# Rotary embedding on one core: the adds of five pieces moved from TensorE to VectorE, and pieces of 6, 5 and 5 positions in place of 4

## The chip, the cores and the metric

The kernel runs on one core of a Trainium2 chip. The metric is device microseconds from launch to end; the profile's span, from the first to the last instruction, is about 1.8 us shorter. Runs are sorted into fast and slow ones: a run more than 1.5% above the fastest of its kernel counts as slow.

## The reference

```python
# x: (8, 2048, 8, 64) float32; cos, sin: (2048, 32) float32
x1 = x[..., :32]
x2 = x[..., 32:]
out1 = x1 * cos - x2 * sin        # cos, sin broadcast over batch and heads
out2 = x1 * sin + x2 * cos
return np.concatenate([out1, out2], axis=-1)
```

Every element is read once and written once, 33.55 MB each way, for three arithmetic operations per output element: two products and an add.

## The kernel before

Each of the 128 partitions holds 16 consecutive sequence positions, so one batch is a tile of 128 x 8192 elements, 512 (8 heads of 64) per position. Five such tiles are kept (`NBUF = 5`), and the result is written over the input. A tile is worked on in pieces of a few positions. SBUF and PSUM are two on-chip memories: the tiles lie in SBUF, and TensorE's results go to PSUM. In most pieces (kind A) GpSimd multiplies the swapped halves by the signed sines (`t2`), VectorE multiplies by the cosines (`t1`, in PSUM), and VectorE adds. To relieve VectorE, three pieces (kind B) are added on TensorE: two matmuls with the identity into one PSUM bank (the tile `o` of 512 elements), copied out ("evicted") by ScalarE. To relieve GpSimd too, two pieces (kind C) take both products on VectorE and the add on TensorE.

```python
kinds = {}
for b, kind in ((1, "C"), (2, "B"), (3, "C"), (4, "B"), (5, "B")):
    kinds[(b, 0)] = kind
# ...
if kind != "C":
    keep(nc.gpsimd.tensor_mul(out=t2..., in0=swapped(xt, nr), in1=signed(sgn[...], nr)))
keep(nc.vector.tensor_mul(out=t1..., in0=xk, in1=rep(cos_ps[...], 2 * H)))
if kind == "A":
    keep(nc.vector.tensor_add(out=xt, in0=t1, in1=t2))
elif kind == "B":
    for j in range(n // C):
        o = o_pool.tile([P, C], f32, tag="o")
        cs = slice(j * C, (j + 1) * C)
        nc.tensor.matmul(o, eye, t1[:, cs], start=True, stop=False)
        nc.tensor.matmul(o, eye, t2[:, cs], start=False, stop=True)
        keep(nc.scalar.copy(xt[:, cs], o))
# ... kind C: second product on VectorE, then as B with +-identity

# per batch: pieces of 4 positions ([2, 2, 4, 4, 4] in the first, [4, 4, 4, 2, 2] in the last),
# one store per batch (three in the first and the last: 8, 4, 4 positions), then:
if b + NBUF <= last:
    load(b + NBUF)          # waits until the store of batch b has landed
```

Of the kernel before, what the change touches and what calls it, by code (L numbers as in the profile page):

```python
# [9 lines left out]
@with_exitstack  # L10
def kernel(
    ctx: ExitStack,
    tc: tile.TileContext,
    x: bass.AP,
    cos: bass.AP,
    sin: bass.AP,
    out: bass.AP,
):
    nc = tc.nc
    keep = tc.keep_in_program_order  # L20
    f32 = mybir.dt.float32
    PSUM = bass.MemoryType.PSUM

    B, S, H, D = x.shape
    Dh = D // 2
    P = 128
    HD = H * D
    R = S // P
    ROW = R * HD
    UNIT = 4 * HD  # L30
    NBUF = 5
    C = 512
    last = B - 1

    xv = x.rearrange("b (q r) h d -> b q (r h d)", q=P)
    ov = out.rearrange("b (q r) h d -> b q (r h d)", q=P)
    cos_src = cos.rearrange("(q r) d -> q r d", q=P)
    sin_src = sin.rearrange("(q r) d -> q r d", q=P)

    const_pool = ctx.enter_context(tc.tile_pool(name="const", bufs=1))  # L40
    tab_pool = ctx.enter_context(tc.tile_pool(name="tab", bufs=1, space=PSUM))
    t1_pool = ctx.enter_context(tc.tile_pool(name="t1p", bufs=1, space=PSUM))
    o_pool = ctx.enter_context(tc.tile_pool(name="op", bufs=2, space=PSUM))
    t1s_pool = ctx.enter_context(tc.tile_pool(name="t1s", bufs=2))
    xpool = ctx.enter_context(tc.tile_pool(name="xpool", bufs=NBUF))
    t2_pool = ctx.enter_context(tc.tile_pool(name="t2p", bufs=3))

    cos_sb = t1s_pool.tile([P, R, Dh], f32, tag="t1s", name="cos_sb")
    sin_sb = t1s_pool.tile([P, R, Dh], f32, tag="t1s", name="sin_sb")
    sgn = const_pool.tile([P, R, 2, Dh], f32, tag="sg")  # L50
    eye = const_pool.tile([P, P], f32, tag="eye")
    neye = const_pool.tile([P, P], f32, tag="neye")
    cos_ps = tab_pool.tile([P, R, Dh], f32, tag="cp")
    sin_ps = tab_pool.tile([P, R, Dh], f32, tag="sp")

    xts = {}

    def spans(sizes):
        lo = 0
        for n in sizes:  # L60
            yield lo, n
            lo += n

    def load(b):
        xt = xpool.tile([P, ROW], f32, tag="xt", name=f"xt{b}")
        for lo, n in spans([UNIT, UNIT, 2 * UNIT] if b == 0 else [ROW]):
            keep(nc.sync.dma_start(out=xt[:, lo : lo + n], in_=xv[b, :, lo : lo + n]))  # L67
            if b == 0 and lo == 0:
                keep(nc.sync.dma_start(out=cos_sb, in_=cos_src))  # L69
                keep(nc.sync.dma_start(out=sin_sb, in_=sin_src))  # L70
        xts[b] = xt

    def store(b, lo, n):
        keep(nc.scalar.dma_start(out=ov[b, :, lo : lo + n], in_=xts[b][:, lo : lo + n]))  # L74

    for b in range(NBUF):
        load(b)

    nc.gpsimd.memset(eye, 0.0)  # L79
    nc.gpsimd.affine_select(  # L80
        out=eye,
        in_=eye,
        compare_op=mybir.AluOpType.not_equal,
        fill=1.0,
        base=0,
        pattern=[[-1, P]],
        channel_multiplier=1,
    )
    for lo, hi in ((0, 4), (4, R)):
        keep(nc.scalar.mul(sgn[:, lo:hi, 0, :], sin_sb[:, lo:hi, :], -1.0))  # L90
        keep(nc.scalar.copy(sgn[:, lo:hi, 1, :], sin_sb[:, lo:hi, :]))  # L91
    keep(nc.scalar.copy(sin_ps, sin_sb))  # L92
    keep(nc.scalar.mul(neye, eye, -1.0))
    keep(nc.vector.tensor_copy(cos_ps, cos_sb))  # L94

    def rep(a, n):
        return dataclasses.replace(a, ap=[a.ap[0][:], a.ap[1][:], [0, n], a.ap[-1][:]])

    def swapped(a, nr):
        return dataclasses.replace(  # L100
            a,
            offset=a.offset + Dh,
            ap=[a.ap[0][:], [HD, nr], [D, H], [-Dh, 2], [1, Dh]],
        )

    def signed(a, nr):
        return dataclasses.replace(
            a, ap=[a.ap[0][:], [D, nr], [0, H], [Dh, 2], [1, Dh]]
        )

    kinds = {}
    for b, kind in ((1, "C"), (2, "B"), (3, "C"), (4, "B"), (5, "B")):
        kinds[(b, 0)] = kind

    def rotate(b, lo, n):
        kind = kinds.get((b, lo), "A")
        xt = xts[b][:, lo : lo + n]
        r0 = lo // HD
        nr = n // HD
        xk = xt.rearrange("p (r k d) -> p r k d", r=nr, d=Dh)  # L120
        xu = xt.rearrange("p (g u d) -> p g u d", u=2, d=Dh)
        if kind == "A":
            t1 = t1_pool.tile([P, n], f32, tag="t1")
        else:
            t1 = t1s_pool.tile([P, n], f32, tag="t1s")
        if kind == "C":
            t2 = t1s_pool.tile([P, n], f32, tag="t1s")
        else:
            t2 = t2_pool.tile([P, n], f32, tag="t2")
        t1u = t1.rearrange("p (g u d) -> p g u d", u=2, d=Dh)  # L130
        t2u = t2.rearrange("p (g u d) -> p g u d", u=2, d=Dh)
        if kind != "C":
            keep(
                nc.gpsimd.tensor_mul(  # L134
                    out=t2.rearrange("p (r h u d) -> p r h u d", r=nr, h=H, u=2),
                    in0=swapped(xt, nr),
                    in1=signed(sgn[:, r0 : r0 + nr, :, :], nr),
                )
            )
        keep(  # L140
            nc.vector.tensor_mul(  # L141
                out=t1.rearrange("p (r k d) -> p r k d", r=nr, d=Dh),
                in0=xk,
                in1=rep(cos_ps[:, r0 : r0 + nr, :], 2 * H),
            )
        )
        if kind == "A":
            keep(nc.vector.tensor_add(out=xt, in0=t1, in1=t2))  # L148
        elif kind == "B":
            for j in range(n // C):  # L150
                o = o_pool.tile([P, C], f32, tag="o")
                cs = slice(j * C, (j + 1) * C)
                nc.tensor.matmul(o, eye, t1[:, cs], start=True, stop=False)  # L153
                nc.tensor.matmul(o, eye, t2[:, cs], start=False, stop=True)  # L154
                keep(nc.scalar.copy(xt[:, cs], o))  # L155
        else:
            keep(
                nc.vector.tensor_mul(  # L158
                    out=t2.rearrange("p (r k d) -> p r k d", r=nr, d=Dh),
                    in0=xk,  # L160
                    in1=rep(sin_ps[:, r0 : r0 + nr, :], 2 * H),
                )
            )
            G = C // Dh
            for u in range(2):
                for j in range(n // 2 // C):
                    o = o_pool.tile([P, C], f32, tag="o")
                    gs = slice(j * G, (j + 1) * G)
                    nc.tensor.matmul(o, eye, t1u[:, gs, u, :], start=True, stop=False)  # L169
                    nc.tensor.matmul(  # L170
                        o, eye if u else neye, t2u[:, gs, 1 - u, :], start=False, stop=True
                    )
                    keep(
                        nc.scalar.copy(  # L174
                            xu[:, gs, u, :], o.rearrange("p (g d) -> p g d", d=Dh)
                        )
                    )

    def pieces(b):
        if b == 0:  # L180
            return [2 * HD, 2 * HD, UNIT, UNIT, UNIT]
        if b == last:
            return [UNIT, UNIT, UNIT, 2 * HD, 2 * HD]
        return [UNIT] * 4

    def shares(b):
        if b == 0:
            return [HD, 7 * HD, 2 * UNIT]
        if b == last:
            return [2 * UNIT, UNIT, UNIT]  # L190
        return [ROW]

    for b in range(B):
        done = 0
        outs = list(spans(shares(b)))
        for lo, n in spans(pieces(b)):
            rotate(b, lo, n)
            done = lo + n
            while outs and sum(outs[0]) <= done:
                store(b, *outs.pop(0))  # L200
        if b + NBUF <= last:
            load(b + NBUF)

# [29 lines left out]
```

## Time and profile before

| | before |
|---|---|
| time, median of 3 | 163.44 us (163.41 to 163.58) |
| span of the profiled run | 161.6 us |
| DMA, two queues | 49.7% + 48.3% of the 16 engines' span |
| VectorE busy | 140.1 us (87%) |
| GpSimd busy | 135.8 us (84%) |
| TensorE, ScalarE busy | 47.1 us, 15.1 us |

Three rows are close together. The DMA has the fullest row.

### The profile page before, as it was taken

How to read it: one execution, taken by the hardware profiler on the slowest of the kernel's cores; microseconds unless marked ns; L12 is line 12 of the kernel's file. 1: busy time of each engine (PE TensorE's matmuls, PEld its weight loads, DVE VectorE, ACT ScalarE, POOL GpSimd, SP SyncE). 2: the span in 40 equal slices, each digit the busy share in tenths (PEclk: the TensorE clock that was granted, in tenths of full speed). 3: DMA queues.
4: the chain of work that ended last, by engine and by line, in shares of the span. 5: the costliest groups of instructions: out<-in, count | busy, mean ns of one | idle time of the engine just before them, and what ended most of it. 6: DMA issues, size and time to landing. Idle time of an engine off the chain costs nothing.

```text
span 161.6 us, 440 instructions
## 1 busy us (share of the span) xinstructions
PE 47.1 (29%) x80; PEld 18.7 (12%) x80; DVE 140.1 (87%) x66; ACT 15.1 (9%) x27; POOL 135.8 (84%) x38
## 2 busy tenths in 40 slices
PE   0000000499008940895029901991000000000000
PEld 0000000134003410331014301340000000000000
DVE  0458999999999999999999899999999998999900
ACT  3310000012100220022001300121000000000000
POOL 1199999999999799989995989997999969999100
PEclk9999999999855898579556995599755555555555
DMA  5999999899999999999999998999999999999994
GB/s 187 418 438 482 463 397 390 373 426 507 397 389 450 426 487 389 446 462 389 446 462 389 462 448 381 487 422 389 487 422 397 479 422 397 479 422 397 430 400 209
DMA packets 3457, 67.64 MB, mean 419 GB/s; under 512 B 384, under 2 KB 384, under 8 KB 768
## 3 DMA queue, kind: packets, MB, share of 16 engines
q1 hardware_dynamic: 1728, 34.08, 49.7%
q10 hardware_dynamic: 1728, 33.56, 48.3%
q14 instruction: 1, 0.01, 0.0%
HBM read 34.08 MB, written 33.55 MB: 419 GB/s over the span
## 4 chain that ended last, share of the span: by engine, by line
DMA 46%; DVE 36%; POOL 8%; issue 4%; SPq 1%; ACT 0%; DVEq 0%; POOLq 0%; ACTq 0%
DMA xt<-in_x_dram 24%; DVE t L141 19%; DMA out_dram<-xt 18%; DVE xt L148 16%; POOL t L134 8%; DMA sin_sb<-in_sin_dram 3%; DVE t L158 1%; SPq L69 0%; SPq L67 0%; ACT sgn L91 0%; DVEq L148 0%; ACT sgn L90 0%; POOLq L134 0%; ACTq L74 0%
## 5 line engine op out<-in xcount | busy, mean ns | idle before, releaser
L134 POOL TENSOR_TENSOR t<-xt,sgn 128x2048 f32<-128x2048 f32 (+1 forms) x32 | 135.1, 4253 | 13.5 <-ACT sgn L91 6.0
L141 DVE TENSOR_TENSOR t<-xt,cos_ps 128x2048 f32<-128x2048 f32 (+1 forms) x34 | 73.4, 2166 | 0.8
L148 DVE TENSOR_TENSOR xt<-t,t 128x2048 f32<-128x2048 f32 (+1 forms) x29 | 62.2, 2144 | 6.3 <-POOL t L134 3.4
L153 PE MATMUL o<-t,eye 128*128 128x512 f32 x24 | 16.1, 759 | 24.7 <-DVE t L141 24.7
L169 PE MATMUL o<-t,eye 128*128 128x512 f32 x16 | 11.8, 844 | 37.6 <-DVE t L141 37.6
L154 PE MATMUL o<-t,eye 128*128 128x512 f32 x24 | 14.9, 709 | 0.0
L155 ACT COPY xt<-o 128x512 f32<-128x512 f32 x12 | 7.0, 586 | 45.0 <-PE o L154 45.0
L153 PEld LDWEIGHTS o<-t,eye 128*128 128x128 f32 x24 | 5.8, 255 | 33.0 <-issue 33.0
L174 ACT COPY xt<-o 128x512 f32<-128x512 f32 x8 | 4.7, 586 | 44.6 <-DVE t L141 26.0
L169 PEld LDWEIGHTS o<-t,eye 128*128 128x128 f32 x16 | 3.8, 256 | 42.5 <-POOL t L134 30.6
L154 PEld LDWEIGHTS o<-t,eye 128*128 128x128 f32 x24 | 5.4, 227 | 7.8 <-issue 7.8
L94 DVE COPY cos_ps<-cos_sb 128x512 f32<-128x512 f32 x1 | 0.7, 694 | 6.1 <-DMA cos_sb<-in_cos_dram 6.1
L170 PE MATMUL o<-t,neye 128*128 128x512 f32 x8 | 5.7, 830 | 0.2 <-DVE t L158 0.2
L158 DVE TENSOR_TENSOR t<-xt,sin_ps 128x2048 f32<-128x2048 f32 x2 | 4.6, 2279 | 0.0
L170 PE MATMUL o<-t,eye 128*128 128x512 f32 x8 | 4.1, 592 | 0.0
L170 PEld LDWEIGHTS o<-t,neye 128*128 128x128 f32 x8 | 2.2, 294 | 4.7 <-issue 4.7
L170 PEld LDWEIGHTS o<-t,eye 128*128 128x128 f32 x8 | 1.5, 190 | 1.9 <-issue 1.9
L90 ACT ACT_TABLE_LOAD x1 | 1.3, 1283 | 0.7 <-PEq L217 0.7
L90 ACT ACTIVATE sgn<-sin_sb 128x128 f32<-128x128 f32 (+1 forms) x2 | 0.8, 413 | 4.8 <-DMA sin_sb<-in_sin_dram 4.8
L91 ACT COPY sgn<-sin_sb 128x128 f32<-128x128 f32 (+1 forms) x2 | 0.8, 388 | 0.0
L92 ACT COPY sin_ps<-sin_sb 128x512 f32<-128x512 f32 x1 | 0.6, 577 | 0.0
L79 POOL MEMSET eye<- 128x128 f32 x1 | 0.2, 206 | 0.3 <-POOLq L217 0.3
(6 smaller groups left out, 1.0 us busy)
## 6 DMA issues: line engine op xcount, KB each, us to landing
xt<-in_x_dram SPq DMA_DIRECT2D x7, 4096.0 KB, 39.1
out_dram<-xt ACTq DMA_DIRECT2D x6, 4096.0 KB, 28.2
out_dram<-xt ACTq DMA_DIRECT2D x2, 2048.0 KB, 19.0
xt<-in_x_dram SPq DMA_DIRECT2D x2, 1024.0 KB, 5.9
xt<-in_x_dram SPq DMA_DIRECT2D x1, 2048.0 KB, 11.4
out_dram<-xt ACTq DMA_DIRECT2D x2, 1024.0 KB, 8.8
out_dram<-xt ACTq DMA_DIRECT2D x1, 1792.0 KB, 20.4
cos_sb<-in_cos_dram SPq DMA_DIRECT2D x1, 256.0 KB, 4.9
```

What stands on the lines that cost most here:

```text
L90: keep(nc.scalar.mul(sgn[:, lo:hi, 0, :], sin_sb[:, lo:hi, :], -1.0))
L91: keep(nc.scalar.copy(sgn[:, lo:hi, 1, :], sin_sb[:, lo:hi, :]))
L134: nc.gpsimd.tensor_mul(out=t2.rearrange("p (r h u d) -> p r h u d", r=nr, h=H, u=2), in0=swapped(xt, nr), in1=signed(sgn[:, r0 : r0 + nr, ...
L141: nc.vector.tensor_mul(out=t1.rearrange("p (r k d) -> p r k d", r=nr, d=Dh), in0=xk, in1=rep(cos_ps[:, r0 : r0 + nr, :], 2 * H),)
L148: keep(nc.vector.tensor_add(out=xt, in0=t1, in1=t2))
L153: nc.tensor.matmul(o, eye, t1[:, cs], start=True, stop=False)
L154: nc.tensor.matmul(o, eye, t2[:, cs], start=False, stop=True)
L155: keep(nc.scalar.copy(xt[:, cs], o))
L158: nc.vector.tensor_mul(out=t2.rearrange("p (r k d) -> p r k d", r=nr, d=Dh), in0=xk, in1=rep(sin_ps[:, r0 : r0 + nr, :], 2 * H),)
L169: nc.tensor.matmul(o, eye, t1u[:, gs, u, :], start=True, stop=False)
L170: nc.tensor.matmul(o, eye if u else neye, t2u[:, gs, 1 - u, :], start=False, stop=True)
L174: nc.scalar.copy(xu[:, gs, u, :], o.rearrange("p (g d) -> p g d", d=Dh))
```

## The change

The intent is a simpler kernel: no TensorE part at all, hence no identity matrices, no second table and no eviction. What TensorE's sums and the second table held of PSUM then goes to VectorE's product, which can cover up to 6 positions, so a batch takes three pieces rather than four, with fewer instructions in all. Two of the five pieces (kind C) also give their second product back to GpSimd.

```diff
-    for b, kind in ((1, "C"), (2, "B"), (3, "C"), (4, "B"), (5, "B")):
-        kinds[(b, 0)] = kind
...
-        if kind == "A":
-            keep(nc.vector.tensor_add(out=xt, in0=t1, in1=t2))
-        elif kind == "B":
-            for j in range(n // C):
-                ...
-                nc.tensor.matmul(o, eye, t1[:, cs], start=True, stop=False)
-                nc.tensor.matmul(o, eye, t2[:, cs], start=False, stop=True)
-                keep(nc.scalar.copy(xt[:, cs], o))
-        else: ...
+        keep(nc.vector.tensor_add(out=xt, in0=t1, in1=t2))
...
+    loads = {0: [4, 4, 8]}
+    pieces = {0: [2, 2, 4, 4, 4]}                       # all others: [6, 5, 5]
+    stores = {0: [1, 7, 8], last: [6, 5, 5]}            # all others: one store
```

More of the change, by code (lines that the diff above doesn't have):

```diff
@@ L29 @@
     ROW = R * HD
-    UNIT = 4 * HD
     NBUF = 5
-    C = 512
     last = B - 1
@@ L42 @@
     t1_pool = ctx.enter_context(tc.tile_pool(name="t1p", bufs=1, space=PSUM))
-    o_pool = ctx.enter_context(tc.tile_pool(name="op", bufs=2, space=PSUM))
-    t1s_pool = ctx.enter_context(tc.tile_pool(name="t1s", bufs=2))
     xpool = ctx.enter_context(tc.tile_pool(name="xpool", bufs=NBUF))
     t2_pool = ctx.enter_context(tc.tile_pool(name="t2p", bufs=3))
-    cos_sb = t1s_pool.tile([P, R, Dh], f32, tag="t1s", name="cos_sb")
-    sin_sb = t1s_pool.tile([P, R, Dh], f32, tag="t1s", name="sin_sb")
+    cos_sb = const_pool.tile([P, R, Dh], f32, tag="cb")
+    sin_sb = const_pool.tile([P, R, Dh], f32, tag="sb")
     sgn = const_pool.tile([P, R, 2, Dh], f32, tag="sg")
-    eye = const_pool.tile([P, P], f32, tag="eye")
-    neye = const_pool.tile([P, P], f32, tag="neye")
     cos_ps = tab_pool.tile([P, R, Dh], f32, tag="cp")
-    sin_ps = tab_pool.tile([P, R, Dh], f32, tag="sp")
-    xts = {}
+    loads = {0: [4, 4, 8]}
+    pieces = {0: [2, 2, 4, 4, 4]}
+    stores = {0: [1, 7, 8], last: [6, 5, 5]}
     def spans(sizes):
@@ L62, in spans @@
             lo += n
+    xts = {}
     def load(b):
         xt = xpool.tile([P, ROW], f32, tag="xt", name=f"xt{b}")
-        for lo, n in spans([UNIT, UNIT, 2 * UNIT] if b == 0 else [ROW]):
-            keep(nc.sync.dma_start(out=xt[:, lo : lo + n], in_=xv[b, :, lo : lo + n]))
+        for lo, n in spans(loads.get(b, [R])):
+            cs = slice(lo * HD, (lo + n) * HD)
+            keep(nc.sync.dma_start(out=xt[:, cs], in_=xv[b, :, cs]))
             if b == 0 and lo == 0:
@@ L71, in load @@
         xts[b] = xt
-    def store(b, lo, n):
-        keep(nc.scalar.dma_start(out=ov[b, :, lo : lo + n], in_=xts[b][:, lo : lo + n]))
     for b in range(NBUF):
         load(b)
-    nc.gpsimd.memset(eye, 0.0)
-    nc.gpsimd.affine_select(
-        out=eye,
-        in_=eye,
-        compare_op=mybir.AluOpType.not_equal,
-        fill=1.0,
-        base=0,
-        pattern=[[-1, P]],
-        channel_multiplier=1,
-    )
     for lo, hi in ((0, 4), (4, R)):
@@ L91 @@
         keep(nc.scalar.copy(sgn[:, lo:hi, 1, :], sin_sb[:, lo:hi, :]))
-    keep(nc.scalar.copy(sin_ps, sin_sb))
-    keep(nc.scalar.mul(neye, eye, -1.0))
     keep(nc.vector.tensor_copy(cos_ps, cos_sb))
-    def rep(a, n):
-        return dataclasses.replace(a, ap=[a.ap[0][:], a.ap[1][:], [0, n], a.ap[-1][:]])
-    def swapped(a, nr):
-        return dataclasses.replace(
-            a,
-            offset=a.offset + Dh,
-            ap=[a.ap[0][:], [HD, nr], [D, H], [-Dh, 2], [1, Dh]],
-        )
@@ L106, in signed @@
-    def signed(a, nr):
-        return dataclasses.replace(
-            a, ap=[a.ap[0][:], [D, nr], [0, H], [Dh, 2], [1, Dh]]
-        )
-    kinds = {}
-    for b, kind in ((1, "C"), (2, "B"), (3, "C"), (4, "B"), (5, "B")):
-        kinds[(b, 0)] = kind
-    def rotate(b, lo, n):
-        kind = kinds.get((b, lo), "A")
-        xt = xts[b][:, lo : lo + n]
-        r0 = lo // HD
-        nr = n // HD
-        xk = xt.rearrange("p (r k d) -> p r k d", r=nr, d=Dh)
-        xu = xt.rearrange("p (g u d) -> p g u d", u=2, d=Dh)
-        if kind == "A":
-            t1 = t1_pool.tile([P, n], f32, tag="t1")
-        else:
-            t1 = t1s_pool.tile([P, n], f32, tag="t1s")
-        if kind == "C":
-            t2 = t1s_pool.tile([P, n], f32, tag="t1s")
-        else:
-            t2 = t2_pool.tile([P, n], f32, tag="t2")
-        t1u = t1.rearrange("p (g u d) -> p g u d", u=2, d=Dh)
-        t2u = t2.rearrange("p (g u d) -> p g u d", u=2, d=Dh)
-        if kind != "C":
-            keep(
-                nc.gpsimd.tensor_mul(
-                    out=t2.rearrange("p (r h u d) -> p r h u d", r=nr, h=H, u=2),
-                    in0=swapped(xt, nr),
-                    in1=signed(sgn[:, r0 : r0 + nr, :, :], nr),
-                )
@@ new lines, in rotate @@
+    def rotate(b, lo, n):
+        xt = xts[b][:, lo * HD : (lo + n) * HD]
+        t1 = t1_pool.tile([P, n * HD], f32, tag="t1")
+        t2 = t2_pool.tile([P, n * HD], f32, tag="t2")
+        part = xt.ap[0]
+        swapped = dataclasses.replace(
+            xt,
+            offset=xt.offset + Dh,
+            ap=[part[:], [HD, n], [D, H], [-Dh, 2], [1, Dh]],
+        )
+        s = sgn[:, lo : lo + n, :, :]
+        signed = dataclasses.replace(
+            s, ap=[s.ap[0][:], [D, n], [0, H], [Dh, 2], [1, Dh]]
+        )
+        c = cos_ps[:, lo : lo + n, :]
+        cosines = dataclasses.replace(
+            c, ap=[c.ap[0][:], c.ap[1][:], [0, 2 * H], c.ap[-1][:]]
+        )
+        keep(
+            nc.gpsimd.tensor_mul(
+                out=t2.rearrange("p (r h u d) -> p r h u d", r=n, h=H, u=2),
+                in0=swapped,
+                in1=signed,
@@ L139, in rotate @@
             )
+        )
         keep(
             nc.vector.tensor_mul(
-                out=t1.rearrange("p (r k d) -> p r k d", r=nr, d=Dh),
-                in0=xk,
-                in1=rep(cos_ps[:, r0 : r0 + nr, :], 2 * H),
-            )
-        )
-        if kind == "A":
-            keep(nc.vector.tensor_add(out=xt, in0=t1, in1=t2))
-        elif kind == "B":
-            for j in range(n // C):
-                o = o_pool.tile([P, C], f32, tag="o")
-                cs = slice(j * C, (j + 1) * C)
-                nc.tensor.matmul(o, eye, t1[:, cs], start=True, stop=False)
-                nc.tensor.matmul(o, eye, t2[:, cs], start=False, stop=True)
-                keep(nc.scalar.copy(xt[:, cs], o))
-        else:
-            keep(
-                nc.vector.tensor_mul(
-                    out=t2.rearrange("p (r k d) -> p r k d", r=nr, d=Dh),
-                    in0=xk,
-                    in1=rep(sin_ps[:, r0 : r0 + nr, :], 2 * H),
-                )
-            )
-            G = C // Dh
-            for u in range(2):
-                for j in range(n // 2 // C):
-                    o = o_pool.tile([P, C], f32, tag="o")
-                    gs = slice(j * G, (j + 1) * G)
-                    nc.tensor.matmul(o, eye, t1u[:, gs, u, :], start=True, stop=False)
-                    nc.tensor.matmul(
-                        o, eye if u else neye, t2u[:, gs, 1 - u, :], start=False, stop=True
-                    )
-                    keep(
-                        nc.scalar.copy(
-                            xu[:, gs, u, :], o.rearrange("p (g d) -> p g d", d=Dh)
-                        )
-                    )
@@ L179, in pieces @@
-    def pieces(b):
-        if b == 0:
-            return [2 * HD, 2 * HD, UNIT, UNIT, UNIT]
-        if b == last:
-            return [UNIT, UNIT, UNIT, 2 * HD, 2 * HD]
-        return [UNIT] * 4
-    def shares(b):
-        if b == 0:
-            return [HD, 7 * HD, 2 * UNIT]
-        if b == last:
-            return [2 * UNIT, UNIT, UNIT]
-        return [ROW]
+                out=t1.rearrange("p (r k d) -> p r k d", r=n, d=Dh),
+                in0=xt.rearrange("p (r k d) -> p r k d", r=n, d=Dh),
@@ L193 @@
+                in1=cosines,
+            )
+        )
+        keep(nc.vector.tensor_add(out=xt, in0=t1, in1=t2))
     for b in range(B):
-        done = 0
-        outs = list(spans(shares(b)))
-        for lo, n in spans(pieces(b)):
+        outs = list(spans(stores.get(b, [R])))
+        for lo, n in spans(pieces.get(b, [6, 5, 5])):
             rotate(b, lo, n)
-            done = lo + n
-            while outs and sum(outs[0]) <= done:
-                store(b, *outs.pop(0))
+            while outs and sum(outs[0]) <= lo + n:
+                so, sn = outs.pop(0)
+                cs = slice(so * HD, (so + sn) * HD)
+                keep(nc.scalar.dma_start(out=ov[b, :, cs], in_=xts[b][:, cs]))
```

## The prediction

> **What bounds the kernel now.** I read, in this order, the page's busy rows and DMA rows, the groups by form, the chain that ended last, the VectorE timeline near the end, and a table of windows over the tail. First the page:
>
> ```profile
> PE 47.1 (29%) x80; PEld 18.7 (12%) x80; DVE 140.1 (87%) x66; ACT 15.1 (9%) x27; POOL 135.8 (84%) x38
> ...
> DMA  5999999899999999999999998999999999999994
> ...
> HBM read 34.08 MB, written 33.55 MB: 419 GB/s over the span
> ```
>
> No compute engine is the bound over the whole span. The DMA row is: 8 or 9 tenths in every slice but the first and the last. 67.63 MB at the 425 to 431 GB/s that the windows below show need about 158 us of a 161.6 us span. TensorE, which the change removes, is at 29%. VectorE and GpSimd are close behind the DMA, so each has some 20 us to lose before it sets the end, less its start and its tail. Now the costs, from the groups by form (instructions, busy us, mean ns):
>
> ```profile
> L134 POOL TENSOR_TENSOR t<-xt,sgn 128x2048 f32<-128x2048 f32 x28 | 125.9, 4525 | 7.4 <-DVE xt L148 3.8 <-DMA xt<-in_x_dram 3.7
> L141 DVE TENSOR_TENSOR t<-xt,cos_ps 128x2048 f32<-128x2048 f32 x30 | 68.5, 2291 | 0.7
> L148 DVE TENSOR_TENSOR xt<-t,t 128x2048 f32<-128x2048 f32 x25 | 57.3, 2291 | 4.3 <-POOL t L134 1.7 <-DVE t L141 0.5
> L134 POOL TENSOR_TENSOR t<-xt,sgn 128x1024 f32<-128x1024 f32 x4 | 9.3, 2346 | 6.0 <-ACT sgn L91 6.0
> L141 DVE TENSOR_TENSOR t<-xt,cos_ps 128x1024 f32<-128x1024 f32 x4 | 4.9, 1229 | 0.1
> ```
>
> The two sizes give each engine a straight line: VectorE 1.06 us per 1024 elements plus 0.17 us, GpSimd 2.18 us plus 0.17 us. The chain that ended last (start us, us, what):
>
> ```profile
> 63.03 29.52 DMA out_dram<-xt
> ...
> 92.62 39.10 DMA xt<-in_x_dram
> ...
> 131.85 4.52 POOL t L134
> 136.37 0.02 issue
> 136.39 2.30 DVE xt L148
> ...
> 152.09 1.22 DVE xt L148
> ```
>
> The load of the last batch waits for the store of batch 2 (five input buffers), lands at 131.7 us, and only then can GpSimd start the last batch. Its adds end at 153.3, and 8.3 us follow. Those 8.3 us are a backlog of stores, not one store:
>
> ```profile
> 131.70:139.30 7.60, 0.00 (x0) 0.00 (x0) 6.99 (x4) 0.00 (x0) 7.45 (x2) 0.50 1.00 431
> 139.30:153.35 14.05, 0.00 (x0) 0.00 (x0) 13.50 (x8) 0.00 (x0) 10.62 (x4) 0.50 0.96 415
> 153.35:159.00 5.65, 0.00 (x0) 0.00 (x0) 0.00 (x0) 0.00 (x0) 0.00 (x0) 0.50 0.99 420
> 159.00:161.60 2.60, 0.00 (x0) 0.00 (x0) 0.00 (x0) 0.00 (x0) 0.00 (x0) 0.50 0.20 82
> ```
>
> (The last two columns are DMA share and GB/s.) From 153.35 to 159.0 the engines move 5.65 x 420 = 2.37 MB at full rate, though the last store has only 1.05 MB: when VectorE finishes, about 1.5 MB of older stores is still queued. The shortest landing of any store is 7.4 us, and it is this one, so it lands near 160.7, and about 0.9 us of ending follows. So today VectorE could be some 3 us later at the end without much harm, and no more.
>
> **What the Trainium skill says.** "VectorE: DVE Perf Modes", section "Mode 2×_2P", says fp32 tensor_tensor stays at one element per cycle, and its section "Side-by-side: where the cycles go for N=2048 bf16" gives a constant of about 150 cycles per instruction and 2293 ns for 2048 elements at that rate. The trace agrees: 2291 ns and a constant of 0.17 us. So a larger tile saves a constant, nothing per element. "GPSIMD Engine Reference", section 3.1, has 4497 ns for the same two-input operation on GpSimd; the trace has 4525. "SBUF — State Buffer", section "SBUF: two separate sides", says that a VectorE operation with two SBUF inputs excludes a GpSimd operation that reads SBUF for its whole length. In both kernels every VectorE product reads one operand from SBUF and the cosines from PSUM, and every VectorE add takes the product from PSUM, so the lock should not appear; in the trace both engines are at 9 tenths together and keep their lone durations, which agrees. "DMA: Bandwidth & Descriptors", section "Anatomy of one DMA", fits about 2 us of fixed cost to each DMA (there for DMAs issued by GpSimd), most of it the wait for the write's receipt; the trace shows 4.7 us for the first 1 MB load, against 2.5 us of data at 420 GB/s, so about 2.2 us.
>
> **The change, part by part.** *Removed:* 80 matmuls, 20 ScalarE evictions, the identity matrices, the second table. All are beside the path (TensorE and ScalarE wait most of the time), so this saves nothing directly. The GpSimd set-up of the identity ends at 1.3 us, long before GpSimd starts at 7.35. *Moved to VectorE:* five pieces had their add on TensorE. Three of these (batches 2, 4, 5) gain an add of 2.29 us each on VectorE. The other two (batches 1 and 3) did both products on VectorE and none on GpSimd: there VectorE swaps a product for an add at the same price, and GpSimd gains a product of 4.5 us each. *Larger tiles:* batches 1 to 7 have three pieces in place of four (batch 7 had five).
>
> VectorE's timeline gives a period for a product plus its add, gaps included:
>
> ```profile
> 138.72 2.30 DVE L141 TENSOR_TENSOR t<-xt,cos_ps 128x2048 f32<-128x2048 f32 x1
> 141.12 2.29 DVE L148 TENSOR_TENSOR xt<-t,t 128x2048 f32<-128x2048 f32 x1
> 143.44 2.30 DVE L141 TENSOR_TENSOR t<-xt,cos_ps 128x2048 f32<-128x2048 f32 x1
> ```
>
> That is 143.44 - 138.72 = 4.72 us for 2048, and in the same view 150.76 - 148.17 = 2.59 us for 1024. The line through them gives 6.86 us for 3072 elements (6 positions) and 5.79 us for 2560 (5 positions), so a batch takes 6.86 + 2 x 5.79 = 18.44 us on VectorE. Before, a batch with all adds on it took 4 x 4.72 = 18.9, one with an add on TensorE 16.6. On GpSimd: 6.70 + 2 x 5.61 = 17.9 us, below VectorE.
>
> Batch 0 is untouched, and VectorE leaves it at 28.28 as now. GpSimd leaves it at 25.3 and has its first 3072 product by about 32.0; VectorE would want it at 31.75, so 0.3 us is lost there; after that GpSimd gains on it. No load is late: batches 2, 4, 6 and 7 had landed by 39.2, 73.1, 112.5 and 131.7, and VectorE now comes to them at about 47, 84, 121 and 139. It therefore runs without waits to 28.28 + 0.3 + 7 x 18.44 = **157.7 us**, 4.3 us later than now.
>
> Then the stores. The store queue is still FIFO-bound in the middle: loads are let go every 19.4 us (53.83, 73.27, 92.62), each by a store that was issued 25 us or more before it landed, so issuing batch 2's store 2.5 us later is absorbed. At 139.3 all loads and the stores of batches 0 to 5 (59.25 MB) have been moved: 131.7 x 425 + 7.6 x 431 = 59.25. Batch 6's store is issued at 28.6 + 6 x 18.44 = 139.2, just in time. It takes 9.9 us, to about 150; the three last stores of 1.57, 1.31 and 1.31 MB are issued at 146.1, 151.9 and 157.7 and need 3.7, 3.1 and 3.1 us. The first two are through by about 157, so the last finds the queue empty: its 2.2 us of fixed cost is no longer hidden. It lands at 157.7 + 5.3 = 163.0, and with 0.9 us of ending the span is 163.9, 2.3 us more than 161.6. The time follows the span: 163.44 + 2.2 = **165.6 us** (+1.3%).
>
> **The rivals.** *A: the DMA hides it all.* The bytes are the same and the DMA row is full, so if about 1 MB of backlog is still there at 157.7 (a lower rate in the middle would do that), the end stays near 161.6 to 162.5: 163.5 to 164.3 us. For it: 98% DMA share. Against: 59.25 MB against 139.2 leaves no slack. *B: VectorE or GpSimd is later than the sum.* If the three GpSimd buffers make it wait so that VectorE waits for its product in every batch, 0.2 to 0.3 us a batch, the end goes to about 167.5. Against: GpSimd is 0.5 us per batch faster, and a GpSimd piece (6.7) is shorter than the two pairs and a product that VectorE has meanwhile. *C: faster.* Fewer instructions and semaphores on all engines give back 0.5 us per batch on the plain batches. That is already in the 18.44, and the DMA floor near 158 us plus start and end leaves under 1 us to gain: 162.5 at best.
>
> **Range and chances.** The terms that are unsure are VectorE's end (about 0.5 us), the lone store's landing (4.7 to 6 us) and backlog. 80%: 164.2 to 166.8. The 2% line is at 166.7, so 0.10 slower; faster than 160.2 is under the DMA floor, 0.01; within 2% 0.89.
>
> **What would show it.** VectorE's busy time should be near 145.7 us and GpSimd's near 144; VectorE's last add should end near 157.7, with no wait on GpSimd above a few tenths after batch 1; the 128x3072 product should take 3.35 us on VectorE and 6.7 us on GpSimd. The last store should land in 5 to 6 us instead of 7.4, and the DMA share should dip before it. The chain should run back through VectorE adds and products to the start, not through the load of the last batch. The prediction is wrong if the chain still goes through that load, if VectorE waits on GpSimd in each batch, or if the last store still meets a backlog.

## The result, and the profile after

The changed kernel took 164.78 to 164.90 us in its four fast runs; two more, of 170.7 us, count as slow and are left out, as are the slow runs of the kernel before. The ratio to the kernel before is 1.0084 (95% interval 1.0064 to 1.0104). A ratio here compares the fast runs of two kernels in the same rounds, so it is not quite the ratio of the medians quoted. The change costs 0.8%, inside the 2% that counts as the same.

The page of the changed kernel, busy row, DMA row and chain by engine:

```profile
DVE 145.5 (89%) x53; ACT 2.6 (2%) x5; POOL 142.5 (87%) x30
...
DMA  5999998999899989999999899899999999998956
...
DVE 76%; POOL 13%; issue 3%; DMA 3%; SPq 0%; DVEq 0%; ACT 0%
```

VectorE has 5.4 us more work with 13 instructions fewer, GpSimd 6.7 us more with 8 fewer. The chain that ended last is now VectorE's own: 76% of the span, where before it was DMA 46% and VectorE 36%. At the right end of the DMA row stand a 5 and a 6 where the kernel before had 9 and 4.

The groups by form (count, busy us and mean ns of one, idle before):

```profile
L98 POOL TENSOR_TENSOR t<-xt,sgn 128x2560 f32<-128x2560 f32 x14 | 78.1, 5600 | 0.0
L98 POOL TENSOR_TENSOR t<-xt,sgn 128x3072 f32<-128x3072 f32 x7 | 46.8, 6681 | 0.1
L105 DVE TENSOR_TENSOR t<-xt,cos_ps 128x2560 f32<-128x2560 f32 x14 | 39.6, 2828 | 0.5
L105 DVE TENSOR_TENSOR t<-xt,cos_ps 128x3072 f32<-128x3072 f32 x7 | 23.5, 3361 | 0.2
```

The waits. Apart from 0.2 us before a constant is set up, these are the only ones on GpSimd and VectorE:

```profile
POOL t L98 <- ACT sgn L76: 7.0, 1, 7.0
DVE cos_ps L77 <- DMA cos_sb<-in_cos_dram: 6.2, 1, 6.2
...
DVE xt L111 <- POOL t L98: 2.7, 3, 1.7
```

After the first 7 us no compute engine is shown waiting for a load. GpSimd runs from 7.4 to 149.8 us with no gap over 0.1 us. VectorE waits three times for it, twice in batch 0 as before and once at batch 1 (0.44 us), and then never again. In the kernel before, GpSimd stood still for loads four times, 3.7 us in all, the last times near 112 and 131 us.

The chain in order of time (start us, us, what), from its last GpSimd piece to its end:

```profile
25.41 6.69 POOL t L98
32.11 0.02 issue
32.13 3.37 DVE xt L111
...
154.86 2.83 DVE xt L111
```

And the tail in windows (start and end, length, busy us of VectorE, ScalarE and GpSimd, granted clock, DMA share, GB/s):

```profile
131.70:139.30 7.60, 7.43 (x4) 0.00 (x0) 7.50 (x3) 1.00 1.00 431
139.30:157.00 17.70, 17.33 (x6) 0.00 (x0) 10.52 (x2) 1.00 0.95 407
157.00:158.00 1.00, 0.69 (x1) 0.00 (x0) 0.00 (x0) 1.00 0.02 10
158.00:161.50 3.50, 0.00 (x0) 0.00 (x0) 0.00 (x0) 1.00 0.90 374
```

To 139.3 us the DMA does what it did before (431 GB/s in the same window). Then it runs dry: between 157 and 158 us it moves 10 GB/s while VectorE finishes its last add at 157.7. The last store, 1.31 MB, starts on an idle DMA and lands 4.5 us later, at 162.2. Before, the last store met a queue, and the DMA was at 420 GB/s to 159.0.

### The profile page after: what moved, and what is told of

It is laid out like the page before. It is cut to its first block, busy times and chain, and to the rows that moved or that the text cites. A ratio compares the mean times of both kernels' runs of the same rounds, so it can differ in the third digit from the quotient of the medians.

```text
span 163.0 us, 217 instructions
## 1 busy us (share of the span) xinstructions
DVE 145.5 (89%) x53; ACT 2.6 (2%) x5; POOL 142.5 (87%) x30
## 4 chain that ended last, share of the span: by engine, by line
DVE 76%; POOL 13%; issue 3%; DMA 3%; SPq 0%; DVEq 0%; ACT 0%
DVE xt L111 39%; DVE t L105 37%; POOL t L98 13%; DMA sin_sb<-in_sin_dram 3%; DVEq L111 0%; SPq L67 0%; SPq L65 0%; ACT sgn L76 0%; ACT sgn L75 0%
## 5 line engine op out<-in xcount | busy, mean ns | idle before, releaser
L98 POOL TENSOR_TENSOR t<-xt,sgn 128x2560 f32<-128x2560 f32 (+3 forms) x26 | 142.3, 5516 | 7.1 <-ACT sgn L76 7.0
L111 DVE TENSOR_TENSOR xt<-t,t 128x2560 f32<-128x2560 f32 (+3 forms) x26 | 72.4, 2784 | 5.1 <-POOL t L98 2.7
L105 DVE TENSOR_TENSOR t<-xt,cos_ps 128x2560 f32<-128x2560 f32 (+3 forms) x26 | 72.5, 2787 | 0.9
## 6 DMA issues: line engine op xcount, KB each, us to landing
out_dram<-xt ACTq DMA_DIRECT2D x6, 4096.0 KB, 26.5
```

The costliest lines, as they stand in the source:

```text
L98: nc.gpsimd.tensor_mul(out=t2.rearrange("p (r h u d) -> p r h u d", r=n, h=H, u=2), in0=swapped, in1=signed,)
L105: nc.vector.tensor_mul(out=t1.rearrange("p (r k d) -> p r k d", r=n, d=Dh), in0=xt.rearrange("p (r k d) -> p r k d", r=n, d=Dh), in1=cosines,)
```

## The experiments

The theory: VectorE's unbroken chain from the end of batch 0, plus one lone store, sets the end, a little above a floor that the DMA sets for both kernels. The rivals: the DMA alone sets the end whatever VectorE does; GpSimd or its buffers make VectorE late; the cost lies in the middle. Eight kernels were run, in three sets, each set on one chip together with the kernel before. The changed kernel itself was not run in them: where a run is compared with it, both are taken by their ratio to the kernel before, and by their medians. The run with two buffers, which repeats the changed kernel almost exactly on another chip, has 1.0078 where that has 1.0084. Diffs are against the changed kernel.

### tiles4: TensorE removed, tiles as before

```diff
-    pieces = {0: [2, 2, 4, 4, 4]}
-    stores = {0: [1, 7, 8], last: [6, 5, 5]}
+    pieces = {0: [2, 2, 4, 4, 4], last: [4, 4, 4, 2, 2]}      # all others: [4, 4, 4, 4]
+    stores = {0: [1, 7, 8], last: [8, 4, 4]}
```

> TensorE removed as in the changed kernel, but the tiles of the kernel before (four of 4 positions a batch, the last batch 4, 4, 4, 2, 2 with its stores of 8, 4 and 4 positions). Theory (VectorE's chain from the end of batch 0 plus one lone store sets the end): VectorE needs 4 x 4.725 = 18.9 us a batch and 19.4 in the last, so its last add ends at 28.3 + 6 x 18.9 + 19.4 = 161.1 us; a lone store of 1.05 MB and the ending add about 4.7, so span 165.8 and time 167.6 us, 1.025 of before. Rival (the DMA sets the end, tile sizes are hidden): 164.8 us as the changed kernel, or less.

Measured: 168.04 us, ratio 1.0256 (1.0234 to 1.0278). VectorE's last add ends at 161.5 us, the last store lands 3.8 us later, the span is 166.2. All three are within half a microsecond of the sum. The rival, that the DMA hides VectorE, falls. The change thus has two parts of opposite sign: taking TensorE out costs 2.6%, and the larger pieces give back 1.7 points of it by the ratios (3.2 us of 168, 1.9%, by the medians). VectorE's last add comes 3.8 us earlier with them, where the sums of instruction durations have 3.4 (161.1 against 157.7); 0.7 us of that goes back to the longer landing of the larger last store.

### adds_dropped: VectorE relieved of five adds

```diff
-        keep(nc.vector.tensor_add(out=xt, in0=t1, in1=t2))
+        if not (1 <= b <= 5 and lo == 0):
+            keep(nc.vector.tensor_add(out=xt, in0=t1, in1=t2))
```

> The changed kernel without the add of the first piece of batches 1 to 5; wrong in a third of those batches on purpose. It takes 5 x 3.4 = 17 us of work off VectorE and nothing else. Theory: VectorE stops being the bound, the last batch starts when its load lands near 131.7 us, its last add ends near 153.4, the last store meets a backlog again, and the time falls to that of the kernel before, 163.4 us (0.99 of the changed kernel). Rival (the DMA with this store pattern, or GpSimd with its larger tiles, sets the 164.8): no change.

Measured: 163.45 us, ratio 0.9976 (0.9954 to 0.9999). Its output is wrong, which doesn't matter for the time. With 17 us taken off VectorE, the time falls only to that of the kernel before. The last add ends at 154.4 us and the shortest landing of a store is 6.3 us against 4.5, so the last store has a backlog again: the DMA stays full to 159 us. One detail was expected otherwise: it is not the load that gates the last batch but GpSimd. The window from just before the end of VectorE's last add, and the wait, in this run:

```profile
153.40:159.00 5.60, 1.04 (x1) 0.00 (x0) 0.00 (x0) 1.00 1.00 424
...
DVE xt L112 <- POOL t L98: 17.1, 8, 3.1
```

VectorE now waits 17.1 us for GpSimd, which still runs without a gap to 149.9 us. So GpSimd's chain stands only some 3 us behind VectorE's. It is not alone there: in the changed kernel the last load lands at 131.9 us by the trace's landing records, and GpSimd begins the last batch at 132.0.

### small_tail: a smaller last store

```diff
+    pieces = {0: [2, 2, 4, 4, 4], last: [6, 5, 3, 2]}
+    stores = {0: [1, 7, 8], last: [6, 5, 3, 2]}
```

> The changed kernel with its last batch cut in 6, 5, 3 and 2 positions, each stored at once, so the lone last store is 0.52 MB in place of 1.31 MB. Theory (last add plus a lone store): VectorE ends 0.5 us later, at 158.2; the store of 3 positions goes at 155.6 and the DMA has work until about 158.7; the last 0.52 MB lands near 161, span 161.9, time 163.7 us. Rival (the cost of the change lies in the middle, in waits or a lower DMA rate): 164.8 to 165.3 us.

Measured: 163.69 us, ratio 0.9985 (0.9966 to 1.0005), results right, span 161.9 as expected. VectorE's last add ends later than in the changed kernel (158.1 against 157.7), and still the time is lower than that of the changed kernel, by 1.0% by the ratios and 0.7% by the medians and spans (161.9 against 163.0). The windows of this run, last columns DMA share and GB/s:

```profile
157.00:158.00 1.00, 1.00 (x1) 0.00 (x0) 0.00 (x0) 1.00 0.99 416
158.00:159.00 1.00, 0.13 (x1) 0.00 (x0) 0.00 (x0) 1.00 0.61 246
159.00:160.00 1.00, 0.00 (x0) 0.00 (x0) 0.00 (x0) 1.00 1.03 422
```

The hole between 157 and 158 us is filled by the store of 3 positions; a smaller dip is left between 158 and 159, and the last 0.52 MB lands 2.9 us after its issue. No other part of the kernel was touched, so a change of the tail alone takes back the cost, and this kernel, without TensorE, is level with the kernel before.

### dma_only: no arithmetic

```diff
-            rotate(b, lo, n)
```

> The changed kernel with no arithmetic in the eight batches: every load and store stands, each store waits for its load alone; the output is a copy of the input, wrong on purpose. It measures the DMA floor. Theory: 67.6 MB at 425 to 430 GB/s plus about 1.6 us of start and 2 us of ending, 161 to 163 us, so both kernels stand within 2% of the floor and a change of the arithmetic can gain next to nothing. Rival (the stores are held back by the arithmetic and the floor is far lower): below 155 us.

Measured: 162.99 us, ratio 0.9944 (0.9921 to 0.9966), the output a copy of the input. The middle runs at the same rate as in the changed kernel (432 GB/s from 28.3 to 131.7 us in both):

```profile
28.28:131.70 103.42, 0.00 (x0) 0.00 (x0) 0.00 (x0) 1.00 1.00 432
```

So with these loads and stores no arrangement of the arithmetic should be worth more than about 0.6% (0.3 to 0.8%) against the kernel before.

### two_bufs and sbuf_product: GpSimd's buffers, and why the product lies in PSUM

```diff
-    t2_pool = ctx.enter_context(tc.tile_pool(name="t2p", bufs=3))
+    t2_pool = ctx.enter_context(tc.tile_pool(name="t2p", bufs=2))      # two_bufs, sbuf_product
-    t1_pool = ctx.enter_context(tc.tile_pool(name="t1p", bufs=1, space=PSUM))
+    t1_pool = ctx.enter_context(tc.tile_pool(name="t1p", bufs=1))      # sbuf_product only
```

> The changed kernel with two buffers in place of three for GpSimd's products. GpSimd may then start a piece only when the add two pieces back is done, and VectorE has a pair and a product left then, 5.8 + 2.9 us or more, against GpSimd's 6.7 us at most. Theory: no wait on VectorE, same time, 164.8 us. Rival B of the prediction (GpSimd's buffers make VectorE wait): 166 us or more.

Measured: 164.88 us, ratio 1.0078 (1.0065 to 1.0091), as the changed kernel. GpSimd waits 1.8 us in all for a buffer, VectorE 2.8 us for GpSimd against 2.7 with three. Rival B of the prediction has no footing.

> As the kernel with two buffers, but VectorE's product lies in SBUF in place of the 6 PSUM banks, so each add has two inputs in SBUF. Theory (such an add and a GpSimd product exclude each other for their whole length): a batch costs GpSimd's 17.9 us plus the adds' 9.0 us, 26.9, so 28 + 7 x 26.9, about 217 us and 222 us of time if all of it serialises, and the adds or GpSimd products show as longer than 2.83 and 5.6 us. Rival (no exclusion): 164.8 us.

Measured: 231.43 us, ratio 1.4146 (1.4127 to 1.4164), results right: against the run with two buffers in the same rounds, 40% more for one memory space. Three lines of its timeline (start us, us, then the idle time before in brackets):

```profile
103.49 2.82 DVE L105 TENSOR_TENSOR t<-xt,cos_ps 128x2560 f32<-128x2560 f32 x1
103.53 5.58 POOL L98 TENSOR_TENSOR t<-xt,sgn 128x2560 f32<-128x2560 f32 x1 [3.30 <-DVE xt L111]
106.41 5.39 DVE L111 TENSOR_TENSOR xt<-t,t 128x2560 f32<-128x2560 f32 x1
```

The VectorE product (cosines in PSUM) runs beside GpSimd at its usual 2.82 us. The add, now with both inputs in SBUF, is issued at 106.41, while GpSimd's product runs to 109.11, and shows 5.39 us: 2.70 us of standing still and 2.69 us, about its lone length, of work. In the same run the last add, after GpSimd has finished, takes 2.83 us with both inputs in SBUF, so the memory space alone does not slow it. The standing still is the exclusion that the Trainium skill, "SBUF — State Buffer", section "SBUF: two separate sides", states for such an add and a GpSimd operation that reads SBUF. The period of a batch is 26.67 us (121.26 to 147.93 in VectorE's timeline) against an expected 26.9. The expectation was 9 us short all the same: it forgot that batch 0 serialises too, and VectorE leaves batch 0 at 41.3 us rather than 28.3, of which the last add, with nothing beside it, gives some 3.6 us back.

### two_on_pe: two adds back on TensorE, with one bank

```diff
+    o_pool = ctx.enter_context(tc.tile_pool(name="op", bufs=1, space=PSUM))
-    t2_pool = ... bufs=3
+    t2_pool = ... bufs=2
+        on_pe = (b, lo) in ((2, 6), (4, 6))        # t1 of these from a buffer in SBUF
+        if on_pe:
+            for j in range(n):                      # as kind B of the kernel before
+                ... two matmuls with eye into o, scalar.copy to xt
+        else:
+            keep(nc.vector.tensor_add(out=xt, in0=t1, in1=t2))
```

(with the small tail as well)

> The changed kernel with the small tail (6, 5, 3, 2), two buffers for GpSimd's products, and the adds of the second piece of batches 2 and 4 put back on TensorE with the one PSUM bank that is left, evicted by ScalarE; results right. VectorE sheds 2 x 2.86 = 5.7 us and would end near 152.5, before which the load of the last batch gates it. Theory: the DMA is the bound again, 163.2 us with the time of before as the limit, 162.6 to 163.5. Rival (there is still time to gain on VectorE): below 162 us; or the single bank delays the stores of batches 2 and 4 enough to hold up loads: above 164 us.

Measured: 173.29 us, ratio 1.0592 (1.0577 to 1.0607), results right. A miss, by 10 us. The expectation had named the single bank as a risk, but for the stores; what the trace shows is GpSimd held up. VectorE waits 19.5 us for GpSimd and GpSimd 13.9 us for VectorE. GpSimd's timeline around the first TensorE piece:

```profile
55.51 5.62 POOL L115 TENSOR_TENSOR t<-xt,sgn 128x2560 f32<-128x2560 f32 x1
64.06 6.68 POOL L115 TENSOR_TENSOR t<-xt,sgn 128x3072 f32<-128x3072 f32 x1 [2.94 <-DVE xt L136]
74.22 5.58 POOL L115 TENSOR_TENSOR t<-xt,sgn 128x2560 f32<-128x2560 f32 x1 [3.47 <-DVE xt L136]
```

TensorE's piece, in five rounds through one bank of about 2.7 us each, reads its GpSimd product until about 73 us. With two buffers, that leaves one, as we read it. GpSimd and VectorE then take turns: GpSimd's product ends at 70.74, VectorE's add runs to 74.14, and only then does GpSimd start again, at 74.22.

### two_on_pe_own: the same with buffers of their own

```diff
+        if on_pe:                                   # tiles 6, 4, 6 in batches 2 and 4
+            t1 = own_pool.tile([P, n * HD], f32, tag="own", name="t1o")
+            t2 = own_pool.tile([P, n * HD], f32, tag="own", name="t2o")
```

> The run with two adds on TensorE lost 10 us, and its trace blames GpSimd: with two buffers, one held by TensorE's piece for five rounds of its single PSUM bank, the next product could not start. Here the two moved adds (now pieces of 4 positions, tiles 6, 4, 6 in batches 2 and 4) take both operands from buffers of their own, the rest as there. If the held buffer is the cause: GpSimd runs without a gap from 7.4 to about 150 us, VectorE ends near 154.5 gated by GpSimd, the DMA is the bound, 163.2 to 163.7 us, level with the kernel before. If the slow rounds of the single bank hold up stores and with them loads: 166 us or more.

Measured: 163.58 us, ratio 1.0006 (0.9962 to 1.0051), results right; the interval is wide enough that the comparison counts as unclear. GpSimd has no gap until its last piece. Of the two explanations this is the one of the held buffer, not that of the slow single bank. The two pieces also shrank from 5 to 4 positions here, and the runs do not separate that. VectorE ends at 155.7 us, in place of 158.1 in the run with the small tail alone, and the time does not follow: 161.9 us of span in both. The floor holds (161.1 us of span without arithmetic), and no correct version run here beats the kernel before by a margin that the runs resolve. The run with the small tail is level with the kernel before and far simpler.

## Why the prediction was right

- **VectorE's end.** The sum 28.28 + 0.3 + 7 x 18.44 gave 157.7 us; the trace has 157.7. The period between batches is 18.44 us (47.11 to 65.55), the wait at batch 1 was 0.44 us for 0.3. Straight lines through 1024 and 2048 elements held at 2560 and 3072: 3.36 us on VectorE and 6.68 on GpSimd against 3.35 and 6.7.
- **Busy times.** VectorE 145.5 us for 145.7. GpSimd 142.5 for 144: in the trace its pieces overlap by about 0.05 us at their edges, which busy time counts once. (The 4497 ns that the prediction cites for GpSimd is for an add on that page; here it is a product.)
- **The middle is absorbed.** Batches 1 and 2 are stored later than before (batch 2 at 65.55 in place of 63.03), yet loads are let go at 53.81, 73.18 and 92.56 us, as before to a tenth. Stores take 26.5 us (median of the 4 MB ones) to land there, against 4.5 for the last one alone, so a later issue is taken up in that wait.
- **The tail.** A DMA that runs dry, then a lone store: the windows show it, and the run with the small tail, which changes only the tail, gains 0.7 to 1.0%. The mis-sized term is the lone store's fixed cost. The prediction took 2.2 us from the first load, near the 2 us that it cites from the Trainium skill. But that load shared the DMA with the two tables: until it landed, 1.29 MB had moved and not 1.05, which is 0.6 us of its 2.2. The lone store of 1.31 MB landed in 4.5 us, which at 420 GB/s is 3.1 us of data and 1.4 us of fixed cost. That is the 0.8 us by which the time was overstated (165.6 for 164.84). Two smaller slips are in that sum: a span longer by 2.3 us was entered as 2.2, and the 425 GB/s comes from a row of the windows (0 to 131.7 us) that the prediction does not print.
- **Rival A** (the DMA hides it all) came nearer in time than the forecast (163.5 to 164.3, against 165.6, for 164.84), so the time alone would not have decided. What decides is the DMA at 10 GB/s before the last store, where A needs a backlog. About 3 us of the 4.3 by which VectorE ends later were hidden, and the change used more. **Rival B** fell with the run of two buffers. **Rival C** is bounded by the run without arithmetic.
- **What the prediction did not see.** It compared GpSimd with VectorE per batch only. The run with dropped adds shows that GpSimd would bind next, some 3 us behind. And it checked the loads against VectorE's arrival at a batch (139 for the last), where GpSimd comes first, at 132.0, with the load landed at 131.9. That no load came late for GpSimd is luck; a slightly later load should still have cost nothing, as VectorE takes that product at 142.75 us, 4 us after it is done.

## What to carry to other kernels

When three limits stand within a few microseconds of each other, ask when each engine finishes and what is still queued at that moment, rather than which busy share is the largest: here the former backlog of stores was worth about 3 us of cover for VectorE, and the change spent it. What is left after the last compute instruction is one store's bytes plus a fixed cost, so the last piece should be small. Giving work back to an idle engine is free only if the buffers that it holds are not the ones that the busy engines turn around in.

## What the Trainium skill lacked or had wrong

- "DMA: Bandwidth & Descriptors", section "Anatomy of one DMA": its fixed cost of about 2.0 us is fitted to DMAs that GpSimd issues, and it has no such fit for those of ScalarE. Lone stores issued by ScalarE landed here in 4.5 us for 1.31 MB and 3.8 us for 1.05 MB, which at 420 GB/s leaves 1.4 and 1.3 us. By the trace's packet records some 0.84 us of this lie before the first packet and 0.34 us after the last, where the section, for its path, puts most of the 2 us into the write's receipt.
- "SBUF — State Buffer", section "Summary: rules for kernel authors", advises about 358 GB/s for the end-to-end time of transfers between HBM and SBUF. On this lone core, loads and stores together ran at 432 GB/s over 103 us, with arithmetic and without; 358 would have put the floor far above the measured time (an estimate: 67.6 MB at that rate take 189 us). That row does not tell a lone core from two at once; other pages of the skill do.
- The same page is right on the exclusion of VectorE and GpSimd, but gives no price for a kernel in which both are nearly full. Here it was 231.43 us against 164.88. Nor does any page that was read name the remedy that both kernels use: a VectorE product laid in PSUM, so that the add has one input in SBUF.
